# Priority marks in a build's ordering, and two units of a matmul group by token halves, in a hybrid encoder layer

## The chip, the cores and the metric

The kernel runs on one core of a Trainium2 chip. The metric is the device time of one execution in microseconds. A core has a matmul engine (TensorE; in profiles PE, with its weight loads as PEld), three engines for elementwise work (VectorE = DVE, ScalarE = ACT, GpSimd = POOL) and SyncE (SP), which issues transfers. Each has its own queue of instructions; they meet through semaphores. On-chip memory is SBUF and, for matmul results, PSUM.

## The reference

One encoder layer for 512 prompt and 64 sample tokens (576 columns), model width 1024:

```python
h   = x @ w_in                                   # 3376 columns
mix = concat(forgetting_attention(h), indexed_sparse_attention(h))
x   = layer_norm(ALPHA * x + mix @ w_o)
hid = square(relu(x @ w_up))                     # width 4096
x   = layer_norm(ALPHA * x + hid @ w_down)
x   = x + sigmoid(x @ w_gate + b) * (p @ w_ple)
```

The new keys, values and log gates are returned too. The change touches the two lines with `w_up` and `w_down`.

## The kernel before

**Layout.** Activations lie with features on the partitions: `Y`, `BH`, `BL` are 128 x 8 blocks x 576 tokens. Each f32 matmul is done as three with rounded operands: high weight by high activation, high by low, low by high. So each operand, weight or activation, is *split*: ACT casts the high part, DVE subtracts it to get the low part. For weights these are lines 149 (cast) and 155 (subtraction), for the hidden activations lines 1327 and 1325. The 576 tokens are worked as two halves, A (columns 0 to 287) and B (288 to 575).

**The feed-forward stage** cuts width 4096 into eight groups of 512. `up(g)` computes groups 0 and 1 directly: four weight units of 128 columns, each over all eight feature blocks. In `up(1)` each unit `c` takes both halves in turn, 24 matmuls each, into one PSUM tile; `up_evac` then makes relu and square (lines 1372 and 1373) and, after every second unit, calls `operands`. Groups 2 to 5 up, and groups 0 to 5 down, go through `seven`, a seven-product scheme (Strassen's kind) over 2 x 2 blocks: weight halves against sums and differences of the token and feature quarters. Groups 6 and 7 go up through it too and down directly (`down_last`).

**Seven products.** A *pair* is one 2 x 2 problem: `up_pair(g, m)` or `down_pair(g, c)`. Its products run in the order 11, t0, t1, 21, t3, t2, 22, each 12 matmuls of 288 columns, pinned in that order on PE (line 288). Four PSUM areas hold the sums: `P.o` (11, then t1 and t2 added on top), `P.z` (t0), `P.d` and `P.e` (the other two outputs). Two outputs begin with a copy of what `P.o` holds: after 11, ACT copies `P.o` to `P.d` (line 1464), and t1 may not write `P.o` before that; after t1, ACT writes `-P.o` to `P.e` (line 1468). These are the *seed copies*. After t3 a DVE operation reads `P.e` (line 1517 in up pairs, 1557 in down pairs); product 22 then writes on into `P.e`, so it must wait for that reader.

**Operands of the products.** For the hidden activations the quarters and their sums are named 11, 12, 22, s1, s2, s3, s4 in `HX` (tiles `hA`: 11 and s3, `hB`: 12 and 22, `hC`: s1 and s2, `hD`: s4). `operands(g, m, t, v)` makes them from the squared values of units 2m and 2m+1, half t: for odd g and the second half (t = 1) line 1348 makes s2, line 1350 s1, and 22 is the value itself; for the first half the value is 12, and line 1355 adds to it for s4. Product t1 reads s2, 21 reads 12, t3 reads s1, t2 reads 22, 22 reads s4. Each has four blocks; units 0 and 1 make the first two, units 2 and 3 the last two. For the up pairs the same names are made once from the normalized input by `sums_of_x`; its s4 overwrites blocks 0 to 3 of half B of `BH` and `BL` (lines 1424 and 1426), which `up(1)` reads.

**The order of the list of pairs** is four down pairs of group 1 (a down pair takes its group and the one before), four up pairs of groups 2 and 3, four down pairs of group 3, then the same for 4 and 5, and four up pairs of groups 6 and 7.

**Weights.** Raw weights arrive by transfers issued on SP (line 208), with one addition on POOL's queue per pair (line 210), into four buffers of 1024 columns and one of 512. Of a pair's four split units the second has products t0 and t3, the third t1 and t2, the fourth (512 columns) only 22. Before the third is split, lines 181 and 184 add up its raw weights on DVE. Split units live in five slots; a unit's slot is free when the products that read it are done. `use(u, oldest)` says which is the oldest unit still needed, and splits are written into the program only for units less than five ahead of it.

**What sets the order of the work.** PE's products are pinned; on the other engines the program order comes from `later`, a list of small functions with due times, up to three of which are called after every six matmuls. It is only a first order. When the program is complete, the build goes through it with its own estimate of every instruction's time; an engine that is free then gets, of all its instructions whose inputs are there, the one with the lowest priority number, which is its place in the program. `tc.high_priority()` gives the instructions in its block a number that puts them first among those that are ready. The result is fixed: at run time each engine works through its queue in that order.

Of the kernel before, what the change touches and what calls it, by code (L numbers as in the profile page):

```python
# [8 lines left out]
F32 = mybir.dt.float32  # L9
F32R = mybir.dt.float32r  # L10
AF = mybir.ActivationFunctionType
OP = mybir.AluOpType
# [19 lines left out]
HW = NT // 2  # L32
# [4 lines left out]
def tile_hybrid_step(ctx: ExitStack, tc: tile.TileContext, I, O):  # L37
    nc = tc.nc
    PE, ACT, DVE, POOL, SP = nc.tensor, nc.scalar, nc.vector, nc.gpsimd, nc.sync
# [22 lines left out]
    def later(delay, fn):  # L62
        number[0] += 1
        evq.append((clock[0] + delay, number[0], fn))
# [214 lines left out]
    WT = Weights()  # L279

    def gemm(ps, W, kmap, aH, aL, cols, yield_every=6, first=True, last=True, wc=slice(0, 128), k0=0, more=False,
             pin=False):

        n = len(kmap) * 3
        i = 0
        for kw, ka in enumerate(kmap, k0):
            for w, a in ((0, aH), (0, aL), (1, aH)):
                mm = PE.matmul(ps, W(w, kw, wc), a[:, ka, cols], start=(first and i == 0), stop=(last and i == n - 1),  # L288
                               skip_group_check=more)
                if pin:  # L290
                    tc.keep_in_program_order(mm)
                i += 1
                if i % yield_every == 0:
                    yield 1
# [62 lines left out]
    U = {}  # L357
# [498 lines left out]
    BH = BL = None  # L856
# [197 lines left out]
    for p in range(7):  # L1054
        if p == 1:
# [3 lines left out]
            BH = base.tile([128, 8, NT], F32R, name="BH", tag="BH")  # L1059
            BL = base.tile([128, 8, NT], F32R, name="BL", tag="BL")  # L1060
# [14 lines left out]
    for x, tag in ((0, "k32"), (1, "t2")):  # L1075
        t = sb.tile([128, NT], F32, name="praw", tag=tag)
# [38 lines left out]
    fs = pS.enter_context(tc.tile_pool(name="fs", bufs=1))  # L1115
    pL = ExitStack()
    lnp = [pL.enter_context(tc.tile_pool(name="fl", bufs=1))]
    A, B = slice(0, HW), slice(HW, NT)
# [4 lines left out]
    def psum_g():  # L1123
        turn[0] += 1
        if turn[0] % 3 == 2:
            return psB.tile([128, 2, 512], F32, name="g", tag="g", bufs=1)
        return psM.tile([128, 2, 512], F32, name="g", tag="m", bufs=2)
# [230 lines left out]
        else:  # L1358
            late.append(lambda: split("s4", v, 2))

    def up_evac(g, c, nn, m, sl):
        mv = m[:, :, :HW]
        if nn == 2:
            t = (A, B).index(sl)
            r = lnp[0].tile([128, 2, 320], F32, name="relu", bufs=2)[:, :, :HW]
            out = HX["f"][:, t, c:c + 2]
        else:
            if c % 2 == 0:
                HX["r"] = fs.tile([128, 2, 2, HW], F32, name="r", bufs=2)
            rr = HX["r"]  # L1370
            r = out = rr[:, :, c % 2]
        later(0, lambda: ACT.activation(r, mv, AF.Relu))
        later(0, lambda: ACT.activation(out, r, AF.Square))
        if nn == 2:
            operands(g, c // 2, t, out)
        elif c % 2:
            for t in (1, 0):
                operands(g, c // 2, t, rr[:, t])

    def up(g, lns=None):  # L1380
        sets(g)
        if lns:
            for h in range(2):
                sl = (A, B)[h]
                Ws = [unit_w(U["U", g, c], U["U", g, 0]) for c in range(4)]
                ms = [psum_g() for _ in range(2)]
                for kp in range(4):
                    lns[h].need(kp)
                    for c in range(4):
                        for _ in gemm(ms[c // 2][:, c % 2, :HW], Ws[c], (2 * kp, 2 * kp + 1), BH, BL, sl,  # L1390
                                      first=(kp == 0), last=(kp == 3), k0=2 * kp):
                            WT.step()
                            yield 1
                        if kp == 3 and c % 2:
                            up_evac(g, c - 1, 2, ms[c // 2], sl)
            return
        for c in range(4):
            W = unit_w(U["U", g, c])
            m = psum_g()
            for h in range(2):  # L1400
                for _ in gemm(m[:, h, :HW], W, range(8), BH, BL, (A, B)[h]):
                    WT.step()
                    yield 1
            if c == 1:
                close_norm()
            up_evac(g, c, 1, m, None)

    SX = {}

# [36 lines left out]
    def seven(pairs):  # L1446

        def product(P, n):
            if n == "11":
                P.o = psum_n()[:, :HW]  # L1450
            elif n == "t0":
                P.z = psB.tile([128, 2, 512], F32, name="g", tag="g", bufs=1)[:, 0, :HW]
            while owed.get(ROWS[n]) and P.X is HX:
                pop_now()
            x = P.X[ROWS[n]]
            ps = P.o if n in ("11", "t1", "t2") else P.z if n == "t0" else P.d if n == "21" else P.e
            first = n in ("11", "t0")
            W = WT.quarter(P.u, n, oldest[0])
            for _ in gemm(ps, W, range(4), x[0], x[1], slice(0, HW), first=first, more=not first, pin=True):
                WT.step()  # L1460
                yield 1
            if n == "11":
                P.d = seeds[0][:, 1, :HW]
                ACT.copy(P.d, P.o)
            elif n == "t1":
                seeds[0] = psM.tile([128, 2, 512], F32, name="g", tag="m", bufs=2)
                P.e = seeds[0][:, 0, :HW]
                ACT.mul(P.e, P.o, -1.0)  # L1468
            if n in P.posts:
                P.posts[n]()  # L1470
            if n in last_use:
                oldest[0] = P.u + last_use[n]

        last_use = {"21": 1, "t3": 2, "t2": 3, "22": 4}
        oldest = [pairs[0].u]
        seeds = [psM.tile([128, 2, 512], F32, name="g", tag="m", bufs=2)]
        for P in pairs:
            if P.start:
                P.start()
            for n in ("11", "t0", "t1", "21", "t3", "t2", "22"):  # L1480
                yield from product(P, n)
# [18 lines left out]
    def up_pair(g, m):  # L1500

        P = Pair(U["P", g // 2, g % 2 * 2 + m], SX)
        b = slice(2 * m, 2 * m + 2)
        tt = DVE.tensor_tensor
        if m == 0:
            P.start = lambda: sets(g)

        def target(t):
            return HX["f"][:, t, b] if g < G_DOWN and g % 2 == 0 else P.r[:, t]

        def t0():
            P.r = fs.tile([128, 2, 2, HW], F32, name="r", bufs=2)
            owe(P, lambda: ACT.copy(P.r[:, 1, 0], P.z))

        def t3():
            settle(P)
            tt(P.r[:, 1, 1], P.e, P.r[:, 1, 0], OP.subtract)

        def t2():
            tt(P.r[:, 1, 0], P.o, P.r[:, 1, 0], OP.add)  # L1520
            if g % 2:
                later(0, lambda: DVE.scalar_tensor_tensor(target(1), P.r[:, 1], 0.0, P.r[:, 1], op0=OP.max, op1=OP.mult))
            else:
                later(0, lambda: ACT.activation(P.r[:, 1], P.r[:, 1], AF.Relu))
                later(0, lambda: ACT.activation(target(1), P.r[:, 1], AF.Square))
            operands(g, m, 1, target(1))

        def s21():
            later(0, lambda: ACT.activation(P.r[:, 0, 0], P.d, AF.Relu))

        def s22():
            later(0, lambda: ACT.activation(P.r[:, 0, 1], P.e, AF.Relu))
            later(0, lambda: ACT.activation(target(0), P.r[:, 0], AF.Square))
            operands(g, m, 0, target(0))
        P.posts = {"t0": t0, "21": s21, "t3": t3, "t2": t2, "22": s22}
        return P

    def down_pair(g, c):

        P = Pair(U["Q", g // 2, c], HX)  # L1540
        tt, stt = DVE.tensor_tensor, DVE.scalar_tensor_tensor
        s = ALPHA if g == 1 else 1.0
        y00, y01, y10, y11 = [Y[:, 2 * c + x, t] for x in range(2) for t in (A, B)]

        def begin(y, ps, op):
            if s == 1.0:
                tt(y, y, ps, op)
            else:
                stt(y, y, s, ps, op0=OP.mult, op1=op)

        def t0():
            owe(P, lambda: begin(y01, P.z, OP.add))
            owe(P, lambda: begin(y11, P.z, OP.subtract))

        def t3():
            settle(P)
            tt(y11, y11, P.e, OP.add)

        def t2():
            later(0, lambda: tt(y01, y01, P.o, OP.add))  # L1560

        def s21():
            later(0, lambda: begin(y00, P.d, OP.add))

        def s22():
            later(0, lambda: begin(y10, P.e, OP.add))
        P.posts = {"t0": t0, "21": s21, "t3": t3, "t2": t2, "22": s22}
        return P

# [224 lines left out]
```

## Time and profile before

| | |
|---|---|
| median of 3 runs | 770.28 us (770.26 to 770.62) |
| profiled execution, its own time | 770.57 us |
| its span | 768.9 us |
| PE busy | 751.5 us, 98% |
| DVE, ACT, POOL busy | 581.1, 465.6, 110.5 us |
| `up(0)`, `up(1)` and all of `seven` | about 330 to 687 us |
| PE idle in 330 to 700 us | 370.0 - 364.0 = 6.0 us |
| PE's wait for line 1464 in that stretch | 4.6 us in 4 cases |
| line 1464 | 24 copies, 383 to 406 ns each |

A row of the order of time gives start, length, engine, line, operation, result and operands with shapes, and in brackets how long the engine was idle before and what released it. `xN` is N instructions in a row. A matmul's length in the trace covers its pipeline: consecutive matmuls start 0.13 us apart. `g<-BH,whl` is a matmul into a PSUM tile named g; lines inside helpers (288, 149, 155) serve many callers, so they are told apart by operand and time.

### The profile page before, as it was taken

How to read it: one execution, taken by the hardware profiler on the slowest of the kernel's cores; microseconds unless marked ns; L12 is line 12 of the kernel's file. 1: busy time of each engine (PE TensorE's matmuls, PEld its weight loads, DVE VectorE, ACT ScalarE, POOL GpSimd, SP SyncE). 2: the span in 40 equal slices, each digit the busy share in tenths (PEclk: the TensorE clock that was granted, in tenths of full speed). 3: DMA queues.
4: the chain of work that ended last, by engine and by line, in shares of the span. 5: the costliest groups of instructions: out<-in, count | busy, mean ns of one | idle time of the engine just before them, and what ended most of it. 6: DMA issues, size and time to landing. Idle time of an engine off the chain costs nothing.

```text
span 768.9 us, 14641 instructions
## 1 busy us (share of the span) xinstructions
PE 751.5 (98%) x5679; PEld 730.5 (95%) x5679; DVE 581.1 (76%) x1158; ACT 465.6 (61%) x933; POOL 110.5 (14%) x130
## 2 busy tenths in 40 slices
PE   9999999999999999999999998999989999999997
PEld 7999989998999999999989998999989999999997
DVE  6788888888777767998697579866898657658653
ACT  6579777888667533588554577435763466525451
POOL 7100324344331000100000000000000000010100
PEclk9999999999999999999999999999999999999999
DMA  8537354244323225244537666667666664730001
GB/s 287 172 64 164 111 147 131 91 147 146 106 72 99 83 84 174 94 148 107 125 87 185 152 152 173 143 164 178 155 148 170 151 160 145 269 134 29 29 28 68
DMA packets 38197, 101.35 MB, mean 132 GB/s; under 512 B 6000, under 2 KB 10224, under 8 KB 38000
## 3 DMA queue, kind: packets, MB, share of 16 engines
q1 hardware_dynamic: 34384, 87.61, 37.2%
q0 software_dynamic: 3456, 12.58, 10.2%
q8 instruction: 44, 0.72, 0.4%
q10 hardware_dynamic: 288, 0.22, 0.1%
q14 instruction: 25, 0.20, 0.1%
HBM read 85.26 MB, written 9.54 MB: 123 GB/s over the span
## 4 chain that ended last, share of the span: by engine, by line
PE 75%; DVE 13%; ACT 8%; issue 2%; DMA 1%; ACTq 0%; DVEq 0%
PE g L288 40%; PE m L288 14%; PE n L288 13%; DVE dbias L693 2%; PE T L56 2%; ACT xr L771 2%; ACT whl L149 2%; DVE m L691 1%; PE V L958 1%; DVE whl L155 1%; PE m L452 1%; DVE sP L891 1%; PE m L466 1%; DVE x L774 1%; PE S L883 1%
## 5 line engine op out<-in xcount | busy, mean ns | idle before, releaser
L149 ACT CAST whl<-wraw 128x1024 fp32r<-128x1024 f32 (+2 forms) x190 | 154.8, 828 | 83.3 <-PE g L288 46.8
L155 DVE TENSOR_TENSOR whl<-wraw,whl 128x1024 fp32r<-128x1024 f32 (+2 forms) x158 | 157.7, 1008 | 49.1 <-ACT whl L149 48.5
L288 PE MATMUL m<-AH,whl 128*128 128x288 f32 x736 | 176.7, 307 | 0.0
L288 PE MATMUL g<-BH,whl 128*128 128x288 f32 (+2 forms) x768 | 160.1, 298 | 0.0
L288 PEld LDWEIGHTS m<-AH,whl 128*128 128x128 f32 x736 | 126.4, 188 | 1.7 <-issue 1.0
L288 PEld LDWEIGHTS g<-BH,whl 128*128 128x128 f32 x768 | 125.0, 188 | 1.5 <-DVE whl L155 0.2
L288 PE MATMUL g<-BL,whl 128*128 128x288 f32 (+2 forms) x384 | 113.0, 295 | 0.0
L288 PE MATMUL m<-AL,whl 128*128 128x288 f32 x368 | 108.7, 295 | 0.0
L288 PEld LDWEIGHTS g<-BL,whl 128*128 128x128 f32 x384 | 72.3, 188 | 0.2
L288 PEld LDWEIGHTS m<-AL,whl 128*128 128x128 f32 x368 | 69.5, 189 | 0.6
L210 POOL DMA_DIRECT2D wraw<-in_w_dram x24 | 20.7, 864 | 291.3 <-DMA wraw<-in_w_dram 192.1
L896 ACT ACTIVATE sP<-sP,st 128x128 f32<-128x128 f32 (+4 forms) x72 | 39.4, 549 | 35.5 <-DVE st L891 35.4
L155 POOL TENSOR_TENSOR whl<-wraw,whl 128x512 fp32r<-128x512 f32 x32 | 42.2, 1332 | 90.2 <-ACT whl L149 85.3
L288 PE MATMUL m<-BH,whl 128*128 128x288 f32 x192 | 42.9, 302 | 0.0
L288 PE MATMUL g<-s,whl 128*128 128x288 f32 x288 | 42.1, 295 | 0.0
L288 PE MATMUL n<-BH,whl 128*128 128x288 f32 x192 | 42.0, 294 | 0.0
L288 PEld LDWEIGHTS g<-s,whl 128*128 128x128 f32 x288 | 39.4, 188 | 0.0
L56 PE MATMUL T<-ident,sP 128*128 128x128 f32 (+1 forms) x176 | 31.3, 273 | 1.5 <-DVE sP L905 0.6
L288 PEld LDWEIGHTS m<-BH,whl 128*128 128x128 f32 x192 | 32.0, 188 | 0.5 <-issue 0.3
L1468 ACT ACTIVATE g<-n 128x288 f32<-128x288 f32 x24 | 9.5, 395 | 37.3 <-PE n L288 37.3
L288 PEld LDWEIGHTS n<-BH,whl 128*128 128x128 f32 x192 | 32.0, 188 | 0.0
L288 PE MATMUL m<-BL,whl 128*128 128x288 f32 x96 | 28.3, 294 | 0.0
(323 smaller groups left out, 1625.8 us busy)
## 6 DMA issues: line engine op xcount, KB each, us to landing
wraw<-in_w_dram SPq DMA_DIRECT2D x48, 512.0 KB, 3.9
wraw<-in_w_dram POOLq DMA_DIRECT2D x24, 512.0 KB, 6.0
wraw<-in_w_qkv_dram SPq DMA_DIRECT2D x23, 512.0 KB, 3.6
wraw<-in_w_dram SPq DMA_DIRECT2D x24, 256.0 KB, 4.1
wraw<-in_w_up_dram SPq DMA_DIRECT2D x8, 512.0 KB, 3.6
wraw<-in_w_down_dram SPq DMA_DIRECT2D x8, 512.0 KB, 4.4
wraw<-in_w_gate_dram SPq DMA_DIRECT2D x8, 512.0 KB, 4.7
wraw<-in_w_o_dram SPq DMA_DIRECT2D x8, 384.0 KB, 3.1
```

Source lines behind the costliest of these rows:

```text
L56: PE.transpose(out, in_, ident[:n, :n])
L149: ACT.copy(self.hv[u][:, 0, c], src["tile"][:, c])
L155: eng.tensor_tensor(t[:, 1, c], src["tile"][:, c], f(t[:, 0, c]), OP.subtract)
L210: POOL.dma_start(t[:, :n], it["acc"], accum_op=OP.add)
L288: mm = PE.matmul(ps, W(w, kw, wc), a[:, ka, cols], start=(first and i == 0), stop=(last and i == n - 1), skip_group_check=more)
L452: PE.matmul(mk[:, h, :HW], w0(part, k), a[:, k, h * HW:(h + 1) * HW], start=(k == 0 and i == 0), stop=(k == 7 and i == 2))
L466: PE.matmul(acc[b][:n[b], :304], a[:, k, b * 128:b * 128 + n[b]], ixw(part, k), start=(k == 0 and i == 0), stop=(k == 7 and i == 2))
L691: tc.keep_in_program_order(DVE.max(m, s))
L693: tc.keep_in_program_order(DVE.match_replace(out=s, in_to_replace=m, in_values=s, imm_value=GONE))
L771: q(lambda r=r, s=s: ACT.mul(v2(xr[r * 32:r * 32 + 32]), v[s * 32:s * 32 + 32], sc))
L896: ACT.activation(j["P"], j["P"], AF.Exp, bias=j["st"][:, 0:1], scale=-1.0, accum_out=j["st"][:, 2:3])
L1468: ACT.mul(P.e, P.o, -1.0)
```

## The change

Five places get a priority mark or a new order. The two seed copies, the reader `t3` of up pairs and the reader `t3` of down pairs are put in `with tc.high_priority():`. Their inputs and engines stay. In `up(1)` units 0 and 1 are worked as before; units 2 and 3 are worked together, first both for half B, then both for half A, each half into a PSUM tile of its own, followed at once by that half's relu, square and `operands`. Both units are asked for at the start, with unit 2 as the oldest still needed. `up_evac` is split into `up_half`, for group 0, whose calls make what they made before, and `up_evac`, for units 0 and 1 of group 1.

```diff
+    def up_half(g, c, m, sl):
+        t = (A, B).index(sl)
+        r = lnp[0].tile([128, 2, 320], F32, name="relu", bufs=2)[:, :, :HW]
+        out = HX["f"][:, t, c:c + 2]
+        later(0, lambda: ACT.activation(r, m[:, :, :HW], AF.Relu))
         later(0, lambda: ACT.activation(out, r, AF.Square))
-        if nn == 2:
-            operands(g, c // 2, t, out)
...
+        operands(g, c // 2, t, out)
+
+    def up_evac(g, c, m):
+        if c == 0:
+            HX["r"] = fs.tile([128, 2, 2, HW], F32, name="r", bufs=2)
+        rr = HX["r"]
+        r = rr[:, :, c]
+        later(0, lambda: ACT.activation(r, m[:, :, :HW], AF.Relu))
+        later(0, lambda: ACT.activation(r, r, AF.Square))
+        if c:
             for t in (1, 0):
-                operands(g, c // 2, t, rr[:, t])
+                operands(g, 0, t, rr[:, t])
...
-        for c in range(4):
+        for c in range(2):
             W = unit_w(U["U", g, c])
             m = psum_g()
             for h in range(2):
...
-            up_evac(g, c, 1, m, None)
+            up_evac(g, c, m)
+        Ws = [unit_w(U["U", g, c], U["U", g, 2]) for c in (2, 3)]
+        rr = fs.tile([128, 2, 2, HW], F32, name="r", bufs=2)
+        for t in (1, 0):
+            m = psum_g()
+            for c in range(2):
+                for _ in gemm(m[:, c, :HW], Ws[c], range(8), BH, BL, (A, B)[t]):
+                    WT.step()
+                    yield 1
+            later(0, lambda t=t, m=m: ACT.activation(rr[:, t], m[:, :, :HW], AF.Relu))
+            later(0, lambda t=t: ACT.activation(rr[:, t], rr[:, t], AF.Square))
+            operands(g, 1, t, rr[:, t])
...
                 P.d = seeds[0][:, 1, :HW]
-                ACT.copy(P.d, P.o)
+                with tc.high_priority():
+                    ACT.copy(P.d, P.o)
...
                 P.e = seeds[0][:, 0, :HW]
-                ACT.mul(P.e, P.o, -1.0)
+                with tc.high_priority():
+                    ACT.mul(P.e, P.o, -1.0)
...
             settle(P)
-            tt(P.r[:, 1, 1], P.e, P.r[:, 1, 0], OP.subtract)
+            with tc.high_priority():
+                tt(P.r[:, 1, 1], P.e, P.r[:, 1, 0], OP.subtract)
...
             settle(P)
-            tt(y11, y11, P.e, OP.add)
+            with tc.high_priority():
+                tt(y11, y11, P.e, OP.add)
```

More of the change, by code (lines that the diff above doesn't have):

```diff
@@ L1359, in operands @@
             late.append(lambda: split("s4", v, 2))
-    def up_evac(g, c, nn, m, sl):
-        mv = m[:, :, :HW]
-        if nn == 2:
[L1364 to L1372, printed above, removed]
-        later(0, lambda: ACT.activation(out, r, AF.Square))
-        if nn == 2:
-            operands(g, c // 2, t, out)
-        elif c % 2:
+    def up_half(g, c, m, sl):
[3 more added lines that the diff above has]
+        later(0, lambda: ACT.activation(r, m[:, :, :HW], AF.Relu))
+        later(0, lambda: ACT.activation(out, r, AF.Square))
+        operands(g, c // 2, t, out)
[7 more added lines that the diff above has]
+        if c:
             for t in (1, 0):
-                operands(g, c // 2, t, rr[:, t])
+                operands(g, 0, t, rr[:, t])
     def up(g, lns=None):
@@ L1394, in up @@
                         if kp == 3 and c % 2:
-                            up_evac(g, c - 1, 2, ms[c // 2], sl)
+                            up_half(g, c - 1, ms[c // 2], sl)
             return
-        for c in range(4):
+        for c in range(2):
             W = unit_w(U["U", g, c])
```

## The prediction

> **What bounds the kernel now.** I read the page first, then PE's waits between 330 and 700 us, the answer on line 1464, the table by stretches, and at last the order of work on PE, ACT and DVE around each wait.
>
> ```profile
> PE 751.5 (98%) x5679; PEld 730.5 (95%) x5679; DVE 581.1 (76%) x1158; ACT 465.6 (61%) x933; POOL 110.5 (14%) x130
> ```
>
> TensorE (PE) sets the end: it is 98% busy. The change adds and removes no matmul, so it can only win the time in which PE stands, in the stages that it touches.
>
> ```profile
> PE n L288 <- ACT g L1464: 4.6, 4, 1.4
> ```
> ```profile
>   PEld n L288: 6.1, 6
> ```
> ```profile
> 382.00:399.00 17.00, 15.67 (x114) 14.98 (x113) 16.31 (x25) 10.41 (x16) 0.59 (x1) 1.00 0.16 46
> 455.00:482.00 27.00, 24.72 (x183) 24.14 (x182) 26.15 (x38) 18.30 (x32) 1.70 (x2) 1.00 0.67 156
> ```
>
> Line 1464 is the copy of product 11's sum into a seed. PE's matmuls waited for it 4.6 us in four cases (longest 1.4); the second fence, of the answer on line 1464, has the weight loads that waited for it: 6.1 us, six of 24 copies. In the table the columns after the length are PE, PEld, DVE, ACT, POOL, the granted clock and DMA. PE loses time only in a few stretches, and there VectorE (DVE) is nearly full: 26.15 of 27 us, 16.31 of 17.
>
> I count a loss as the distance between the first matmuls of two successive products, less an undisturbed product's: 464.10 to 466.71 is 2.61 us, where 390.00 to 391.60 is 1.60 (12 matmuls each).
>
> ```profile
> 390.00 1.76 PE L288 MATMUL g<-hC,whl 128*128 128x288 f32 x12
> 391.60 1.76 PE L288 MATMUL n<-hB,whl 128*128 128x288 f32 x12
> ...
> 464.10 1.75 PE L288 MATMUL g<-s,whl 128*128 128x288 f32 x12
> 466.71 1.85 PE L288 MATMUL n<-s,whl 128*128 128x288 f32 x12 [0.86 <-ACT g L1464]
> 468.40 0.29 PE L288 MATMUL g<-BH,whl 128*128 128x288 f32 x1
> ...
> 476.36 1.75 PE L288 MATMUL g<-hA,whl 128*128 128x288 f32 x12
> 479.52 1.86 PE L288 MATMUL n<-hC,whl 128*128 128x288 f32 x12 [1.42 <-ACT g L1464]
> 481.22 0.30 PE L288 MATMUL g<-hB,whl 128*128 128x288 f32 x1
> ```
>
> The wait at 466.71 costs 2.61 - 1.60 = 1.01, and its own product 0.09 more (466.71 to 468.40 is 1.69): **1.10 us**. The one at 479.52 costs 3.16 - 1.60 = 1.56 and 0.10: **1.66 us**. Group 5 repeats both (four waits in the row on L1464).
>
> **The change part by part: the seed copies.** The build keeps no written order on ACT and DVE: a free engine gets, of the instructions whose inputs are there by the build's own times, the one written first. High priority puts an instruction ahead of all others that are ready; it neither waits for nor interrupts anything. So I ask for each wait what stood ahead and was ready.
>
> ```profile
> 464.55 0.67 ACT L1327 CAST hC<-hF 128x576 fp32r<-128x576 f32 x1
> ...
> 466.26 0.40 ACT L1464 COPY g<-n 128x288 f32<-128x288 f32 x1
> ...
> 476.79 0.66 ACT L1327 CAST hB<-r 128x576 fp32r<-128x576 f32 x1
> 477.36 1.25 ACT L1327 CAST hC<-hF 128x576 fp32r<-128x576 f32 x2
> ...
> 479.08 0.39 ACT L1464 COPY g<-n 128x288 f32<-128x288 f32 x1
> ```
>
> Product 11 gave way to t0 at 464.10, so its sum was complete near 464.3; the copy came at 466.26, behind three casts of operands (476.79 to 477.36 is one cast's step, 0.57, and 466.26 - 464.55 is three). With priority it goes at 464.55, or one cast later at 465.12 if the build's times call it unready; either ends (0.40) before t1's turn at 464.10 + 1.60 = 465.70. The 1.10 us go whole. At 479.52 the copy may go after L1533 at 476.79, or one cast later, ahead of t1's turn at 477.96.
>
> Here something is late next: t1 of this pair reads s2, which the previous pair has only just made. Its low part is a DVE subtraction behind one of the hC casts, which the copy now delays by up to its own 0.4 us.
>
> ```profile
> 478.18 1.42 DVE L1325 TENSOR_TENSOR hC<-hF,hC 128x576 fp32r<-128x576 f32 x2
> ```
>
> The first of these two ends near 478.18 + 1.42/2 = 478.9. Six of t1's twelve matmuls (six steps of 0.13 = 0.80 us) read blocks finished a pair earlier and can run before. Three bounds for both waits of one group (2.76 us): all of it, if DVE too runs earlier; if DVE keeps its present times, t1 can start in effect at 478.9 - 0.8 = 478.1 instead of 479.52: 1.4 us; with the 27 - 26.15 = 0.85 us of idle in this stretch used up as PE comes sooner, 1.4 + 0.85 = 2.25. PE's earlier t2 also lets line 1520 go ahead of weight splits, which favours the upper half, and a copy ahead of the cast costs up to 0.4 of it. I take **2.2 us for a group, 4.4 for two**; ends 1.4 and 2.76.
>
> The last two of the six copies:
>
> ```profile
> 626.48 1.76 PE L288 MATMUL g<-s,whl 128*128 128x288 f32 x12
> 628.29 1.85 PE L288 MATMUL n<-s,whl 128*128 128x288 f32 x12
> ```
> ```profile
> 626.70 1.24 ACT L1332 CAST hidE<-r 128x576 fp32r<-128x576 f32 x2
> 627.84 0.40 ACT L1464 COPY g<-n 128x288 f32<-128x288 f32 x1
> ```
>
> This one loses 1.81 - 1.60 = 0.21 us and, as above, 0.09 behind it: 0.30; the sixth, in the next pair, as much. Going ahead of one of the two casts (1.24/2 = 0.6 us) is enough, and hidE is read only by `down_last`, after all the products: **0.6 us**, ends 0 and 0.6. The copies after t1 (line 1468) already go first; nothing for them. Check: 2 x 2.76 + 0.6 = 6.1, the ceiling that line 1464's answer shows.
>
> **The reader of the fifth product** (t3; lines 1517, 1557).
>
> ```profile
> 459.17 0.30 PE L288 MATMUL n<-BH,whl 128*128 128x288 f32 x1
> ...
> 460.81 0.41 PE L288 MATMUL g<-BH,whl 128*128 128x288 f32 x1
> ```
> ```profile
> 459.16 1.23 DVE L155 TENSOR_TENSOR whl<-wraw,whl 128x1024 fp32r<-128x1024 f32 x1 [0.41 <-ACT whl L149]
> 460.31 0.45 DVE L1517 TENSOR_TENSOR r<-g,r 128x288 f32<-128x288 f32 x1
> ```
>
> Product 22 overwrites what L1517 reads; it starts 1.64 us after t2 instead of 1.60, and 0.10 follows as after every wait: 0.14 us; if all twelve pairs with that line lose it, 1.7. But the weight split ahead began at 459.16, before t3's last matmul had ended: DVE was free and the reader not ready, and priority does not reserve an engine. I take **0**; ends 0 and 1.7.
>
> **The token halves** (units 2 and 3 of group 1).
>
> ```profile
> 385.04 0.96 PE L288 MATMUL n<-hC,whl 128*128 128x288 f32 x6
> 386.34 0.40 PE L288 MATMUL n<-hC,whl 128*128 128x288 f32 x1 [0.34 <-ACT hC L1327]
> 387.64 0.93 PE L288 MATMUL n<-hC,whl 128*128 128x288 f32 x5 [0.90 <-DVE hC L1325]
> 388.40 0.29 PE L288 MATMUL g<-hB,whl 128*128 128x288 f32 x1
> ...
> 397.97 2.12 PE L288 MATMUL n<-hC,whl 128*128 128x288 f32 x12
> 399.93 1.76 PE L288 MATMUL g<-hB,whl 128*128 128x288 f32 x12
> ```
> ```profile
> 380.46 1.16 ACT L1424 CAST BH<-xr 128x1152 fp32r<-128x1152 f32 x1 [3.02 <-PE g L288]
> 381.65 1.36 DVE L1426 TENSOR_TENSOR BL<-xr,BH 128x1152 fp32r<-128x1152 f32 x1 [4.06 <-ACT BH L1424]
> ```
>
> The first t1 takes 388.40 - 385.04 = 3.36 us instead of 1.60: 1.76 lost, on s2 again. The second takes 1.96: 0.36, on a weight that DVE's backlog makes late. Matmuls, evictions and operand steps keep count and shape. The group ends two products before the first t1, at 385.04 - 3.20 = 381.8. Its second half's 48 matmuls of units 2 and 3 now come first and end 48 x 0.133 = 6.4 us sooner; so does everything made of that half, s2 among it (five DVE steps of 0.7, half the row at 478.18: 3.5 us). L1424 overwrites four blocks of that half and waits for their last read; it and the 1.36 us of L1426 move forward too, into 3.02 us of idle ACT and 4.06 us of idle DVE. So 4.9 us leave DVE's full stretch: s2, which let PE go on at 387.64, is there at 381.2, 3.8 us before t1, and the backlog ahead of the second t1 is gone. What pays: both units hold their weight slots to the end, so the cast that reused unit 2's slot waits 3.2 us more, to 381.8 - 3.2 = 378.6; its unit serves product 22, whose turn is 381.8 + 6 x 1.6 = 391.4. No instruction and no transfer is added; of the transfers on SP and POOL those behind that unit's 512-column buffer (three loads and a sum for the next pairs) come up to as much later, for weights due eleven us on. **2.1 us**; ends 1.4 (the backlog wait stays or grows) and 2.1.
>
> **Sum**: 2.1 + 4.4 + 0.6 + 0 = 7.1 us. The profiled execution took 770.57 us (span 768.9), 0.29 above the median of 770.28: the same 7.1 off the median gives **763.2**. Ends of the parts: 1.4 + 2.8 + 0 = 4.2 and 2.1 + 5.5 + 0.6 + 1.7 = 9.9: 766.1 to 760.4.
>
> **Against it: a queue that stands.** The answer on line 1464 also has the time that ACT sat idle before the copy, until PE was done:
>
> ```profile
>   PE n L288: 4.5, 9
> ```
>
> In nine of 24 cases ACT already stands before the copy, 0.5 us each: the queue's head waits for PE, and what is behind waits too. The Trainium skill ("TensorE: Matmul & The Clock Gate", Architectural detail) says that ACT and DVE are strict FIFO; this row agrees. By that rule alone an earlier place only adds standing, and the sum would be that of the slower rival below.
>
> **The rivals.** *DVE gives the gain back*: DVE is full around both groups, its weight splits come no sooner, and each group gets only the 0.85 us that DVE has to spare. For it: 26.15 of 27; against it: only s2's chain need be early, and the list lets it pass the splits. 2.1 + 1.7 + 0.6 = 4.4: 765.9. *The readers move too* and all ends are reached: 760.4; against it is the row at 459.16. *The build puts the copies where they were*, because by its times the products end later: 2.1 alone, 768.2; against it: at 464.55 the sum had been there for 0.2 us. *The halves win nothing*, a weight slot being short: 5.0, 765.3. *Slower*: priority puts seeds into ACT's queue ahead of the weight casts of the twelve down pairs, before the product has ended on the chip, and each third weight (cast, then split) is late for t1.
>
> ```profile
> 488.40 2.36 DVE L155 TENSOR_TENSOR whl<-wraw,whl 128x1024 fp32r<-128x1024 f32 x2
> ```
> ```profile
> 490.79 1.77 PE L288 MATMUL n<-hC,whl 128*128 128x288 f32 x12
> ```
>
> The first of these two, the third weight, ends near 489.6, 1.2 us before t1. A copy's 0.4 and the present mean standing of 0.5 stay below; from 1.2 us on each us is paid in all twelve. To lose 1.6 us against a gain of 7.1 takes (7.1 + 1.6)/12 = 0.7 beyond the margin, a delay of 1.9, longer than a product: 771.9.
>
> **How the numbers follow.** Forecast 0.60; DVE gives back 0.15; readers too 0.06; copies stay 0.07; halves nothing 0.05; slower 0.04; nothing that can be told 0.03. A run of this kernel tells 0.2%, 1.5 us, from no change. 768.2 lies near that bound, so half of "copies stay" counts as the same: faster 0.90, same 0.06, slower 0.04. The range runs from 760.8 (the readers' case lies below) to 767.4 (above it lie copies that stay, no gain and slower): 0.20 is left out.
>
> **What would show it.** Right: no L1464 among PE's waits; line 1464 ahead of L1327 near 464.6; t1 of the first down pair in one block of 12 near 385.0; L1424 near 374 (k-blocks 0 to 3 of unit 3's first half are read 12 matmuls before that half ends, 375.4 - 1.6); DVE idle within 382 to 399. The 0.14 us before product 22 remain. Wrong: a new wait on L1325 or L155 longer than 0.7 us in t1 of the first or second down pair; L1517 ahead of its split; or casts of weights behind a standing seed.

## The result and the profile after

| | median us (range) | runs |
|---|---|---|
| before, measured beside it | 770.45 (770.26 to 770.87) | 4 |
| after | 765.34 (765.24 to 766.20) | 4 |

The ratio is 0.9935, with a 95% interval of 0.9918 to 0.9953. The change wins 5.1 us, where the prediction's sum was 7.1 (763.2); its range (760.8 to 767.4) holds the time. The profiled execution of after took 765.42 us (span 763.7), that of before 770.57 (768.9): 5.15 less. Two points in PE's order of time bound the stage that the change touches: the matmuls of line 56 stand ahead of all of it, those of line 1180 behind all of it. First before, then after:

```profile
338.69 0.49 PE L56 MATMUL n<-ident,ln_r 128*128 128x128 f32 x3
...
686.62 0.59 PE L1180 MATMUL n<-ln_s,onesm 128*128 128x256 f32 x2
```
```profile
338.38 0.49 PE L56 MATMUL n<-ident,ln_r 128*128 128x128 f32 x3
...
681.58 0.59 PE L1180 MATMUL n<-ln_s,onesm 128*128 128x256 f32 x2
```

So **the stage** takes 347.9 us before and 343.2 after, 4.7 less. From line 1180 to the last matmul both take 77.4 us. The stage starts 0.3 us earlier in the one profile, though every engine has the same order of work ahead of it; over all kernels below that start lies between 338.3 and 339.1 us. So the stage's length is given beside the medians where two kernels lie close together.

From here on the lines are those of after: the copy of 11 is line 1476, `-P.o` 1481, the up pairs' `t3` reader 1531, the sum and square of the second half 1534 and 1536; the lines up to 1355 keep their numbers (1325, 1327, 1348, 1350, 1355, and 149, 155, 181, 184, 288).

Of after, first PE's waits between 330 and 700 us, then two stretches (columns after the length: PE, PEld, DVE, ACT, POOL, the granted clock, DMA):

```profile
PE n L288 <- DVE whl L155: 1.1, 2, 0.5
PE n L288 <- DVE hC L1325: 0.8, 2, 0.4
```
```profile
382.00:399.00 17.00, 17.00 (x130) 17.00 (x130) 13.57 (x21) 8.43 (x13) 0.88 (x1) 1.00 0.46 118
455.00:482.00 27.00, 26.52 (x197) 25.95 (x196) 26.37 (x39) 18.25 (x30) 1.70 (x2) 1.00 0.59 143
```

The seed copy is gone from PE's waits. Two waits of another kind stand there, each once in group 3 and once in group 5. The first stretch, where PE had 15.67 of 17 us, is now full, and DVE has 3.4 us to spare in it. In the second PE is at 26.52 where it was at 24.72.

**The halves.** PE and ACT around the first down pairs of group 1, in after's order of time:

```profile
384.73 1.76 PE L288 MATMUL n<-hC,whl 128*128 128x288 f32 x12
...
395.89 1.77 PE L288 MATMUL n<-hC,whl 128*128 128x288 f32 x12
```
```profile
373.83 1.16 ACT L1435 CAST BH<-xr 128x1152 fp32r<-128x1152 f32 x1 [0.52 <-PE g L288]
```

Both t1 products are unbroken blocks of 12 matmuls. Line 1435 is the cast that overwrites four blocks of half B (1424 before); it comes at 373.8 instead of 380.5, as forecast ("near 374").

**The seeds of group 3.** ACT's order of time in after around the two copies that stalled:

```profile
462.12 0.40 ACT L1476 COPY g<-n 128x288 f32<-128x288 f32 x1
462.45 1.24 ACT L1327 CAST hC<-hF 128x576 fp32r<-128x576 f32 x2
...
473.25 0.40 ACT L1476 COPY g<-n 128x288 f32<-128x288 f32 x1
473.58 1.25 ACT L1327 CAST hB<-r 128x576 fp32r<-128x576 f32 x2
474.72 1.25 ACT L1327 CAST hC<-hF 128x576 fp32r<-128x576 f32 x2
```

Both copies are ahead of all casts. The 1.10 and the 1.66 us that PE lost on them are gone: from t0's start to t1's it is 1.60 us at the first (461.66 to 463.26) and 1.58 at the second (472.81 to 474.39). What came in their place is in PE's order of time:

```profile
472.81 1.75 PE L288 MATMUL g<-hA,whl 128*128 128x288 f32 x12
474.39 1.46 PE L288 MATMUL n<-hC,whl 128*128 128x288 f32 x7
476.24 0.94 PE L288 MATMUL n<-hC,whl 128*128 128x288 f32 x5 [0.39 <-DVE hC L1325]
477.02 1.76 PE L288 MATMUL g<-hB,whl 128*128 128x288 f32 x12
...
486.59 0.43 PE L288 MATMUL n<-hC,whl 128*128 128x288 f32 x2
487.56 1.60 PE L288 MATMUL n<-hC,whl 128*128 128x288 f32 x10 [0.54 <-DVE whl L155]
489.00 1.76 PE L288 MATMUL g<-hB,whl 128*128 128x288 f32 x12
```

Counted as in the prediction (start of t1 to start of the next product, less 1.60), t1 of the first down pair loses 477.02 - 474.39 - 1.60 = **1.03 us**, t1 of the second 489.00 - 486.59 - 1.60 = **0.81 us**. So a group wins 2.76 - 1.03 - 0.81 = **0.92**, not 2.2. (Group 5 loses 1.02 and 0.79.) DVE's and ACT's rows say what is late:

```profile
473.24 0.75 DVE L1348 SCALAR_TENSOR_TENSOR hF<-hF,r 128x576 f32<-128x576 f32 x1
...
474.58 0.75 DVE L1325 TENSOR_TENSOR hB<-r,hB 128x576 fp32r<-128x576 f32 x1
475.43 1.43 DVE L1325 TENSOR_TENSOR hC<-hF,hC 128x576 fp32r<-128x576 f32 x2
...
483.58 0.68 DVE L184 TENSOR_TENSOR wraw<-wraw 128x512 f32<-128x512 f32 x1
484.18 0.45 DVE L1561 TENSOR_TENSOR Y<-Y,g 128x288 f32<-128x288 f32 x1
484.55 2.96 DVE L155 TENSOR_TENSOR whl<-wraw,whl 128x512 fp32r<-128x512 f32 x3
```
```profile
483.62 2.00 ACT L149 CAST whl<-wraw 128x1024 fp32r<-128x1024 f32 x2 [0.98 <-PE g L288]
```

For the first wait: s2's sum (line 1348) is done at 474.0, but ACT is then at two casts of hB, which nothing needs yet, and takes s2's cast of hC only at 474.72; its subtraction follows at 475.43. PE's weight loads there wait for both, 0.33 us for the cast and 0.60 for the subtraction; the row of the matmuls shows 0.39 only. For the second: the sum of the third weight (L184) comes at 483.58, so of the two casts at 483.62 that of the *next* pair goes first, and of the three splits at 484.55 the one that PE waits for is the last, after the fourth weight and after the next pair's first.

**The last two copies** near 627 and 638 us (0.3 us each) no longer hold PE, and **the readers** of t3 stand where they stood, behind a split:

```profile
434.17 1.23 DVE L155 TENSOR_TENSOR whl<-wraw,whl 128x1024 fp32r<-128x1024 f32 x1 [3.92 <-ACT whl L149]
435.31 0.45 DVE L1531 TENSOR_TENSOR r<-g,r 128x288 f32<-128x288 f32 x1
```

The account of after: halves 2.1, seeds 2 x 0.92 = 1.8, last two copies 0.6, readers 0: 4.5 us, against 4.7 in the stage.

### The profile page after: what moved, and what is told of

It reads as the page before. It is cut to its first block, busy times and chain, and to the rows that moved or that the text cites. A ratio compares the mean times of both kernels' runs of the same rounds, so it can differ in the third digit from the quotient of the medians.

```text
span 763.7 us, 14649 instructions
## 1 busy us (share of the span) xinstructions
PE 750.7 (98%) x5679; PEld 730.9 (96%) x5679; DVE 580.3 (76%) x1158; ACT 465.5 (61%) x933; POOL 111.2 (15%) x130
## 4 chain that ended last, share of the span: by engine, by line
PE 78%; DVE 14%; ACT 6%; issue 2%; DVEq 0%; ACTq 0%
PE g L288 41%; PE m L288 14%; PE n L288 13%; PE T L56 2%; DVE dbias L693 2%; ACT xr L771 2%; DVE whl L155 2%; DVE m L691 1%; PE V L958 1%; ACT whl L149 1%; PE m L452 1%; DVE sP L891 1%; PE m L466 1%; DVE x L774 1%; PE S L883 1%
## 5 line engine op out<-in xcount | busy, mean ns | idle before, releaser
L155 DVE TENSOR_TENSOR whl<-wraw,whl 128x1024 fp32r<-128x1024 f32 (+2 forms) x158 | 157.7, 1008 | 48.5 <-ACT whl L149 47.9
L155 POOL TENSOR_TENSOR whl<-wraw,whl 128x512 fp32r<-128x512 f32 x32 | 42.2, 1334 | 89.1 <-ACT whl L149 84.9
```

Of the source, the lines that this page charges most:

```text
L155: eng.tensor_tensor(t[:, 1, c], src["tile"][:, c], f(t[:, 0, c]), OP.subtract)
```

## Experiments

All of them compute the whole layer. Times are medians of device us; ratios are against the kernel before, measured on the same chip in turn with each. Medians of different series are compared as they stand; that of before lay between 770.27 and 770.50. Line numbers shift by a few with each edit. Where the built order of the instructions settles a question by itself, it is said.

### The two parts alone

**Only the seeds' marks** (the kernel before with the two copies of `seven` marked):

```diff
-                ACT.copy(P.d, P.o)
+                with tc.high_priority():
+                    ACT.copy(P.d, P.o)
...
-                ACT.mul(P.e, P.o, -1.0)
+                with tc.high_priority():
+                    ACT.mul(P.e, P.o, -1.0)
```

> The kernel before with priority on the two seed copies alone. From the changed kernel's trace: the two copies behind casts in each of groups 3 and 5 win 2.76 us less the waits that came in their place (1.03 us on s2 and 0.80 us on a weight), so 0.93 for a group, and 0.6 for the last two copies: 2.5 us, 767.9 us. If the prediction's 2.2 for a group were right and the new waits came from the halves, it would be 5.0 us, 765.4 us.

Measured: 767.87 (767.56 to 768.47), ratio 0.9969 [0.9958, 0.9980]: 2.6 us. **Only the halves** (after with all four marks taken out):

> The changed kernel with no priority mark at all, so only the token halves of units 2 and 3. If the halves win both waits of the first down pairs, as the prediction has it: 2.1 us, 768.3 us, and the seed copies' four long waits stand as before. If they only win the first wait: 1.8 us or less, 768.7 us.

Measured: 768.28 (767.98 to 768.78), ratio 0.9972 [0.9962, 0.9983]: 2.2 us, the prediction's 2.1. PE's waits from 330 to 700 us, first with the seeds' marks alone, then with the halves alone:

```profile
PE n L288 <- DVE hC L1325: 1.7, 3, 0.9
PE n L288 <- DVE whl L155: 1.1, 2, 0.5
PE n L288 <- ACT hC L1327: 0.3, 1, 0.3
```
```profile
PE n L288 <- ACT g L1475: 4.6, 4, 1.4
```

With the seeds alone the four new waits are there already (two of the three on hC, and both on whl; the third on hC and the one on ACT are the wait that the halves remove). So the new waits come from the earlier seeds and not from the halves. The two parts do not touch each other: the stage is 2.6 us shorter with the one, 2.1 with the other, and 4.7 with both.

**Readers.** With the readers' marks alone on the kernel before, the built order is the same on every engine as without them. In after, they move two readers of 24, those of one down pair in each of groups 3 and 5, ahead of an addition to `Y` (0.45 us; not of a subtraction of hD, as was expected):

```diff
-            with tc.high_priority():
-                tt(P.r[:, 1, 1], P.e, P.r[:, 1, 0], OP.subtract)
+            tt(P.r[:, 1, 1], P.e, P.r[:, 1, 0], OP.subtract)
...
-            with tc.high_priority():
-                tt(y11, y11, P.e, OP.add)
+            tt(y11, y11, P.e, OP.add)
```

> The kernel after without the marks on the t3 readers (L1531, L1571), the seed copies' marks and the halves kept: in the built order two readers, one in each of groups 3 and 5, go back behind a subtraction of hD, and nothing else differs. Theory A, as the prediction had it: the marks are worth nothing, 765.3 (765.0 to 765.6). Theory B: the two readers cost what the ten others cost, 0.145 each, and delay the chain to s2 by up to 0.7: 765.6 to 767.

Measured: 765.74 (765.63 to 766.20), ratio 0.9939 [0.9922, 0.9955]. After had 765.34 in another series; the intervals lie on each other, PE's waits are the same two rows, and the stage is 343.2 us in both. No effect can be told, as the prediction took it.

### What sets the new waits: the order of the queues, or a full DVE?

DVE is busy 22.3 of the 22.5 us from 467.0 to 489.5 in after. Two theories were open: *order* (what PE needs stands behind things that it does not need yet) and *capacity* (DVE has no time left, so each wait removed comes back elsewhere; the prediction's rival "DVE gives the gain back").

**Marks on s2's chain** (the second half's sum 1534, its square 1536, the sum 1348, cast and subtraction of s2, all with high priority):

```diff
-            later(0, lambda: DVE.scalar_tensor_tensor(F[0], F[0], -1.0, v, op0=OP.mult, op1=OP.subtract))
+            def s2_sum():
+                with first_of(1):
+                    DVE.scalar_tensor_tensor(F[0], F[0], -1.0, v, op0=OP.mult, op1=OP.subtract)
+            later(0, s2_sum)
```

> The changed kernel with priority also on what makes s2 in odd groups: the addition after t2, relu with square on DVE, the sum for s2, its cast and its subtraction. Order theory (DVE has the time, but works weight splits and other operands ahead of s2): the wait of 1.03 us in the first down pair's t1 goes in groups 3 and 5 and the weight wait of 0.80 us stays as it is: 2 us less than the changed kernel, 763.3 us. Capacity theory (DVE is full from 455 to 487 us and what it does first, something else waits for): the weight wait in the second down pair grows by what the first one wins, to about 1.8 us: no gain, 765.3 us.

Measured: 765.54 (765.35 to 765.71), ratio 0.9938 [0.9921, 0.9954]. This tells neither theory: in the built order nothing differs from after. By the build's times s2's steps were not ready when the engine was given something else, and a mark decides only among what is ready. The run is after a second time, and shows how far a repetition lies off (0.2 us; the stage is 343.2 us again).

**Part of DVE's work on GpSimd** (the fourth weight's split):

```diff
-            self.split(u + 3, r3, [lo], DVE)
+            self.split(u + 3, r3, [lo], POOL)
```

> The changed kernel with the subtraction of every pair's fourth weight unit (512 columns) on GpSimd instead of DVE: 0.6 us less DVE work in each of 24 pairs, 2.4 us between 455 and 487 us; that weight has some 8 us of time. Order theory: s2 still stands behind the 1024-column splits, so at most 0.6 us for a group: 764.1 us or more. Capacity theory: the backlog shrinks by 2.4 us, both waits of a group (1.83 us) go: 3.6 us less, 761.7 us. If GpSimd slows DVE where both work, or delays the additions on its queue, slower than 765.3.

Measured: 767.12 (766.71 to 767.33), ratio 0.9957 [0.9942, 0.9972]: 1.8 us slower than after. Of this the stage holds 0.9 (344.1 us); in the profile 0.5 is a later start of the stage, and why the rest is there no run shows. PE's waits, then POOL and DVE in order of time, in this kernel:

```profile
PE n L288 <- DVE hC L1325: 2.7, 2, 1.4
PE n L288 <- DVE whl L155: 0.6, 2, 0.3
```
```profile
471.12 1.27 POOL L155 TENSOR_TENSOR whl<-wraw,whl 128x512 fp32r<-128x512 f32 x1 [7.33 <-ACT whl L149]
```
```profile
471.11 0.45 DVE L1534 TENSOR_TENSOR r<-n,r 128x288 f32<-128x288 f32 x1
471.48 2.00 DVE L155 TENSOR_TENSOR whl<-wraw,whl 128x1024 fp32r<-128x1024 f32 x1
```

Where the waits arise DVE was not relieved: from 455 to 482 us it is busy 26.42 us, against 26.37 in after. A split that takes 1.22 us in after takes 2.00 while GpSimd's is running; it ends 1.09 us after GpSimd's does (472.39), nearly its whole length later. In the second pair the sum of line 184, which takes 0.68 in after, takes 1.60 in the same way (from 484.23, GpSimd's from 483.99). L1534, one of whose inputs is in PSUM, keeps its 0.45, also where it begins inside GpSimd's split (at 437.35, GpSimd's at 437.32). So the 0.68 us taken off DVE come back as 0.78 of standing, ahead of s2. The Trainium skill ("SBUF — State Buffer", Who interferes with whom) has a rule for this: DVE and GpSimd share a pair of ports under an exclusive lock, and a DVE instruction with two inputs in SBUF contends with a GpSimd instruction that reads SBUF; with at most one, outside its two-port modes, it does not. The trace agrees: 2.00 against 1.22 for the first kind, 0.45 for the second. The run says nothing of the two theories.

**Order by edges instead of marks.** An edge (`issue_after`) puts an instruction behind another in the queue whether that one is ready or not. First, the casts of the sets 12 and 22 behind s2's cast:

```diff
+            def high():
+                with tc.issue_after(s2_cast[g, m]) if n in ("12", "22") else nullcontext():
+                    ins = ACT.copy(HX[n][0][:, b], v)
+                if n == "s2":
+                    s2_cast[g, m] = ins.ins
-            later(d, lambda: ACT.copy(HX[n][0][:, b], v))
+            later(d, high)
```

> The kernel after, with ScalarE's casts of the sets 12 and 22 (hB) of the odd groups queued behind the cast of the set s2 (hC) of the same rows by an edge; no work is added or left out, and unlike in the run with the priorities the built order does change. Theory A (order): the first down pair's t1 waits because hC's cast stands behind two casts of hB on ScalarE (in after: hF ready at 473.99, hC's cast begins at 474.72, its subtraction at 475.43). With hC's cast first that wait goes, 1.03 us for each of groups 3 and 5: 765.3 - 2.1 = 763.3, and the split that the second pair's t1 waits for stays about where it was relative to PE. Theory B (VectorE's capacity): VectorE has no gap from 467 to 490 us, so the split of the weights ends no earlier however the order is; PE gets there 1.03 earlier and waits that much longer: 765.3, with PE's wait on whl up from 0.54 to about 1.5 each.

Then, in place of it, the two sums of raw weights marked to go first:

```diff
             def t1():
-                DVE.tensor_tensor(r2["tile"][:, lo], r2["tile"][:, lo], r1["tile"][:, lo], OP.add)
+                with tc.high_priority():
+                    DVE.tensor_tensor(r2["tile"][:, lo], r2["tile"][:, lo], r1["tile"][:, lo], OP.add)
...
             def t2():
-                DVE.tensor_tensor(r2["tile"][:, hi], r2["tile"][:, hi], r2["tile"][:, lo], OP.add)
+                with tc.high_priority():
+                    DVE.tensor_tensor(r2["tile"][:, hi], r2["tile"][:, hi], r2["tile"][:, lo], OP.add)
```

> The kernel after, with the two sums of the seven-weight units (L181, L184) marked to go first in the build's ordering; same work. In after the second sum stands from 483.58 behind a split that is not urgent, so the split that the second down pair's t1 waits for comes third of three at 486.3. Theory A (order): the weight wait goes, 0.80 us for each of groups 3 and 5, and the first pair's wait stays at 1.03: 765.3 - 1.6 = 763.7. Theory B (capacity): what is moved ahead pushes something else that PE waits for by as much: 765.3, with a new or longer wait on hC or hB.

And both:

> Both edits of the two runs before this one in one kernel: the casts of 12 and 22 behind s2's, and the weight sums first. Theory A (order): both new waits go, 2 x (1.03 + 0.80) = 3.7: 761.7, which is the forecast 763.2 less what the two waits of the kernel before still cost there. Theory B (capacity): VectorE's work between 455 and 490 us is the bound and the waits only change their place: 765.3. Between the two: part of it, with the wait that remains named by PE's waits.

| kernel | median us (range) | ratio [95%] | PE's waits on hC, on whl (330 to 700 us) | loss by starts in group 3: t1 of the first, of the second down pair | stage |
|---|---|---|---|---|---|
| after | 765.34 (765.24 to 766.20) | 0.9935 [0.9918, 0.9953] | 0.8, 1.1 | 1.03, 0.81 | 343.2 |
| s2's cast first | 765.54 (765.26 to 765.75) | 0.9935 [0.9918, 0.9953] | 0.6, 1.8 | 0.56, 1.15 | 343.0 |
| weight sums first | 764.12 (764.06 to 764.21) | 0.9918 [0.9903, 0.9934] | 1.2, 0 | 0.84, 0 | 341.2 |
| both | 762.63 (762.19 to 762.87) | 0.9898 [0.9883, 0.9914] | 0, 0 | 0.19, 0 | 339.9 |

PE with the weight sums first, in order of time:

```profile
474.69 1.10 PE L290 MATMUL n<-hC,whl 128*128 128x288 f32 x7
...
477.13 1.76 PE L290 MATMUL g<-hB,whl 128*128 128x288 f32 x12
```

s2's cast first, alone, looks like capacity: the loss on hC is 0.47 us smaller, PE comes sooner to the weight, which is hardly earlier, and loses 0.34 more there, for next to nothing (0.3 us in the stage, none in the median). The weight sums first, alone, look like order: the loss on the weight goes whole, and that on hC does not grow. The idle time in the row on hC says otherwise (0.8 to 1.2), but by starts the product loses 477.13 - 474.69 - 1.60 = 0.84 instead of 1.03, because in this kernel the weight loads wait for the subtraction only: the cast of hC comes at 474.44 instead of 474.72, ahead of hB's second. The stage is 2.0 us shorter, 1.0 for each group; the median shows 1.2 of it. Both together leave no row at all in PE's waits, with the same work on DVE. PE and DVE in that kernel, in order of time, and its stretch:

```profile
474.90 1.95 PE L290 MATMUL n<-hC,whl 128*128 128x288 f32 x12
...
486.25 1.77 PE L290 MATMUL n<-hC,whl 128*128 128x288 f32 x12
```
```profile
481.95 0.68 DVE L186 TENSOR_TENSOR wraw<-wraw 128x512 f32<-128x512 f32 x1
...
484.78 1.82 DVE L155 TENSOR_TENSOR whl<-wraw,whl 128x1024 fp32r<-128x1024 f32 x2
```
```profile
455.00:482.00 27.00, 27.00 (x203) 26.73 (x202) 26.46 (x40) 18.52 (x31) 1.71 (x2) 1.00 0.64 148
```

The second sum (L186 here) is at 481.95 instead of 483.58, so the third weight's split is the first of the two at 484.78 and done near 485.9, ahead of t1 at 486.25. DVE is as full as in after (26.46 of 27), and PE does not stand. So capacity is not what holds PE in after; order is. Of the 3.7 us that both waits cost in after, 0.2 a group stay in t1 (476.69, the next product's start, - 474.90 - 1.60), so 3.3 should be won, and the stage is 3.3 us shorter (339.9 against 343.2). The medians show 2.7; in the profiles 0.5 us of what is missing is a later start of the stage.

### The readers, really moved

The mark did nothing, so the prediction's bound for the readers (0 to 1.7) stayed open. Here the splits of weights that are written after a reader get an edge behind it:

```diff
-                tt(P.r[:, 1, 1], P.e, P.r[:, 1, 0], OP.subtract)
+                reader[0] = tt(P.r[:, 1, 1], P.e, P.r[:, 1, 0], OP.subtract).ins
...
-                    eng.tensor_tensor(t[:, 1, c], src["tile"][:, c], f(t[:, 0, c]), OP.subtract)
+                    with tc.issue_after(reader[0]) if reader[0] is not None else nullcontext():
+                        eng.tensor_tensor(t[:, 1, c], src["tile"][:, c], f(t[:, 0, c]), OP.subtract)
```

> The kernel after, with VectorE's splits of weights (L155) that are traced behind an up pair's t3 reader queued behind that reader by an edge; same work. In after the mark on the readers moved two of them only; ten still stand behind a split and cost PE 0.145 us each (0.04 at the first matmul of product 22 and 0.10 at the second, 435.82 for one). Theory A: the split ahead is the whole cause: 10 x 0.145 = 1.45, 763.9, and no excess is left at 435.82, 447.10, 458.38 and their like. Theory B: VectorE waits idle for the reader's product and the split then comes late for PE: the gain is lost in a new wait on whl, 765.3 or more.

Measured: 764.43 (764.20 to 764.48), ratio 0.9922 [0.9906, 0.9937]: 0.9 us less than after; the stage is 1.2 shorter (342.0). DVE in this kernel, to be held against the rows at 434.17 above, and PE's waits:

```profile
434.61 0.46 DVE L1534 TENSOR_TENSOR r<-g,r 128x288 f32<-128x288 f32 x1 [4.20 <-PE g L291]
434.98 2.35 DVE L158 TENSOR_TENSOR whl<-wraw,whl 128x1024 fp32r<-128x1024 f32 x2
```
```profile
PE n L291 <- DVE whl L158: 1.1, 2, 0.5
PE n L291 <- DVE hC L1328: 1.1, 2, 0.5
```

DVE now stands idle until the reader's product has ended and does the reader first; none of the ten stalls before product 22 is left in the trace (10 x 0.145 = 1.45). The loss on hC grew from 1.03 to 1.16 in each group, so about 0.3 comes back. Its second theory expected the whole gain to come back, and on the weights; the wait on them is as long as in after.

### All orders together, and the seeds taken back

The three edits (s2's cast first, weight sums first, splits behind the readers) in one kernel:

> The casts of 12 and 22 behind s2's, the weight sums first, and the splits behind the up pairs' t3 readers, in one kernel; no work added or left out. Theory A: PE's excess between 330 and 700 us falls from 2.9 us in the kernel with the first two orders by the ten readers' 0.145 each to about 1.5, and the time from 762.6 to 761.2. Theory B: as where the readers were pinned alone, 0.25 of the 1.45 comes back as a wait on hC in each group, so 761.6 to 761.8; if the two first orders no longer hold with the third, 763 or more.

Measured: 762.11 (761.96 to 762.38), ratio 0.9890 [0.9875, 0.9905]; this is the fastest kernel tried, 3.2 us under after. The last step won 0.5 of 1.45 (0.4 in the stage, 339.6): one wait is back, and t1 of the first down pair loses 0.74 instead of 0.19. Which order brings it back was not tried.

```profile
PE n L293 <- DVE hC L1331: 0.9, 2, 0.5
```

Then the kernel with s2's cast and the weight sums first, but with the two seed copies unmarked as they were before the change:

> The kernel with the casts of 12 and 22 behind s2's and the weight sums first, but the two seed copies left unmarked as before the change. In the built order the first seed of groups 3 and 5 then stands behind three casts (hC, hB, hC; 0.57 each) where it stood behind two before, and the second goes ahead of all casts by itself, because those casts now wait for s2's. Theory A: the first seed's stall is the only one left, 1.10 us as before plus one cast, 1.7 for each group: 762.6 + 3.4 = 766.0. Theory B: the seed was worth both stalls (2.76 a group) whatever the casts do: 762.6 + 5.5 = 768.1.

Measured: 768.84 (768.46 to 769.21), ratio 0.9979 [0.9970, 0.9989]: 6.2 us slower than with the marks (6.4 in the stage, 346.3), more than either theory. Its waits, and ACT's order of time:

```profile
PE n L290 <- ACT g L1483: 1.7, 2, 0.9
PE g L290 <- DVE hB L1328: 1.4, 2, 0.7
PE n L290 <- DVE hC L1328: 1.2, 2, 0.6
```
```profile
462.42 0.66 ACT L1332 CAST hC<-hF 128x576 fp32r<-128x576 f32 x1
462.98 0.68 ACT L1332 CAST hB<-r 128x576 fp32r<-128x576 f32 x1
463.55 0.67 ACT L1332 CAST hC<-hF 128x576 fp32r<-128x576 f32 x1
464.12 0.39 ACT L1483 COPY g<-n 128x288 f32<-128x288 f32 x1
```

The first seed stands behind three casts, as expected, but its stall is no longer than it was behind two (0.85 of wait). What costs more is what follows: without the marks the build also places the down pair's steps otherwise. On DVE a split of weights (475.71) goes ahead of hC's subtraction, and both weight sums (477.52 and 478.79) ahead of hB's, so t1 and product 21 of the first down pair wait for hC and hB (0.6 and 0.7 of idle time, 0.87 and 0.95 by starts). So beside those two orders the seeds' marks are worth 6.2 us, where alone on the kernel before they are worth 2.6. What a mark wins cannot be added up; the build lays out everything behind it anew.

## Why the prediction was right or wrong

- **That PE's standing is what can be won**: right. PE's waits from 330 to 700 us went from 5.8 us (the three rows 4.6, 0.9 and 0.3) to 1.9, which are the two new waits.
- **The halves, 2.1 us**: right. Alone 2.2; both t1 are whole, DVE has 3.4 us idle in the stretch, and the cast that overwrites half B comes at 373.8. The weight slot that is held longer cost nothing that shows.
- **The last two copies, 0.6 us**: right by the trace of after.
- **The readers, 0**: right, and for the reason given (a mark does not hold an engine back). That the stall could be won, though not by a mark, is shown by the run with edges: 0.9 us, 1.2 in the stage.
- **The seeds, 2.2 us for a group: wrong, 0.92.** Both copies went where the prediction put them, and both old stalls went whole. The term that failed is what is late next. Of the three bounds, the middle one (DVE's idle 0.85 us is used up as PE comes sooner: 2.25) was taken, and the whole was reasoned on s2 alone. On s2 the group keeps 2.76 - 1.03 = 1.73, between the lower end of 1.4 and the 2.2 taken: s2's cast still has two casts of hB ahead of it. With both orders changed a group keeps 2.76 - 0.19 = 2.57, so the bound was one of order. And the second pair's third weight, 0.81 us, has no term in the sum at all; the trace of before did show how near it was (the weight 1.2 us ahead of t1, in the slower rival's fence, for the same pair of the list): if PE is to come 2.2 us sooner against a margin of 1.2, the weight must come sooner too, and the sum gives no reason why it should. So 2.2 - 0.92 = 1.28 a group and 2.6 in all were lost here, which is more than the 2.0 us between forecast and result. The 0.92 lies below this term's own lower end of 1.4; the time is inside the range only because the halves and the last two copies came in at their upper ends.
- **The wrong-signs** named both: a new wait on L1325 and one on L155, in t1 of the first and second down pair. The idle time in the row (0.39 and 0.54) is under the 0.7 us set there; the loss by starts (1.03 and 0.81) is over it. A threshold should have been set on the distance of starts.
- **The rival "DVE gives the gain back"** (0.85 a group, 765.9) came nearest to the 0.92 of a group, but its mechanism fell: with the same work on DVE, and it as full, PE waits for nothing in that stage once two orders are changed. The rival "the halves win nothing" has the measured time almost exactly (765.3 against 765.34), and its mechanism fell too: the halves alone win 2.2. Both numbers agree by accident.
- **The rival "slower"**, by copies that hold up ACT's queue, did not come about. ACT's queue stood, but no weight cast came late by it for PE in after, beyond what the two waits above are.

What stays open: 0.2 us of the stage's 4.7, what lets the stage start up to 0.75 us sooner or later in one execution than in another, and the 0.9 us that the run with GpSimd loses outside the stage.

## What to carry to other kernels

When a stall is removed, price the consumer that follows on the same engine, and the one after it: here the two products behind the seeds took back two thirds of the gain. A priority mark in a list-scheduled build decides only among instructions that are ready by the build's own times; where something less urgent is ready sooner, only an edge, or an input made ready sooner, changes the order. And a full engine is not yet a bound: change the order of two things together before you call it capacity, since one alone can look like it when the next wait takes its place. Read what a wait costs from the starts of the products, and compare the stage that was changed; sums of idle time and whole medians hid part of what the weight sums won.

## What was not expected of the hardware

- A split of weights on GpSimd (128 x 512, 1.27 us against 0.68 on DVE) made a DVE split that ran beside it take 2.00 instead of 1.22 us, and a DVE sum 1.60 instead of 0.68; the trace counts the standing as DVE's busy time, so a full DVE in a table of busy time can be one that stands. Where DVE's subtractions came first, GpSimd's split took 3.19 us (380.34 to 383.53).
- A wait on PE costs about 0.25 us more than the idle time in its row: 0.54 of idle stood for 0.81 us between starts (t1 of the second down pair of after), and in the prediction's rows 0.86 for 1.10 and 1.42 for 1.66. Of this 0.16 is the way the trace counts: it has a matmul as 0.29 us long, where the next one can start 0.13 after it, and idle time begins only at the recorded end. Some 0.10 is lost behind the wait: the last ten matmuls of that product take 489.00 - 487.56 = 1.44 instead of ten steps of 0.133. What this 0.10 consists of was not tried.
